# A fused SGU, conformer and SwiGLU block: half 1's group norm centred by rounded parts, first feature tiles in other PSUM banks, row sums by array halves, squares in pairs, and a search over the planner's order

## The chip, the cores and the metric

The kernel runs on one core of a Trainium2 chip. The metric is device time in microseconds of one execution. Four compute engines work side by side, each on an instruction stream of its own: TensorE (PE; its weight loads are listed as PEld), VectorE (DVE), ScalarE (ACT) and GpSimd (POOL). SyncE (SP) issues the transfers. An instruction waits on semaphores for the data or the buffer that it needs, and everything behind it on its engine waits with it.

## The reference

One decoder block for 1024 tokens of width 1024 in float32: two mixers side by side, an output projection, a feed-forward part and a last norm. Cut to what matters here:

```python
cond = silu(c) @ ada_w + ada_b                  # six modulation vectors
h = modulate(rmsnorm(x, norm1_g), shift1, scale1)
u, v, val, gate = split(h @ w_in + b_in)        # 512 columns each
v = layernorm(gelu(v)); w = tril(w_s)           # 8 heads, chunks of 128
y_a = gelu(u) * (einsum('hts,bcshd->bcthd', w, v) + b_s)
y = val * sigmoid(gate)
y = causal_depthwise_conv(y, conv_w, width=31) + conv_b
y_b = silu(layernorm(y in 8 groups of 64 channels))
x = x + gate1 * (concat(rmsnorm(y_a), rmsnorm(y_b)) @ w_out)
h2 = modulate(rmsnorm(x, norm2_g), shift2, scale2)
x = x + gate2 * ((silu(g_ff) * up_ff) @ w_ffn_out)   # g_ff, up_ff = h2 @ w_ffn_in
out = modulate(rmsnorm(x, norm_f_g), shift_f, scale_f)
```

## The kernel before

**Layout.** Activations lie feature-major: eight tiles `x0` to `x7` of 128 features by 1024 tokens, worked on in two halves of 512 tokens, half 0 and half 1. Names carry the half: `pu0_2` is tile 2 of the u projection of half 0.

**Products.** A float32 product is made of three products of rounded operands (fp32r). `weights` and `split` make a rounded copy `hi` on ScalarE (`wh_*`) and the rest, `lo` = raw - hi, on GpSimd or VectorE (`wl_*`). `mm3` (L747 to 749; the same in `product`, L1109) then adds hi x hi, lo x hi and hi x lo in one PSUM bank, each a 512-wide matmul. A few matmuls run on plain float32 operands: the sums of squares, the scale matmuls and the group norm's centring among them.

**Stages.** The first phase multiplies half 0's `h1` with the val and gate weights in eight banks, `p0_0` to `p3_1` (L871 onwards), while weights and modulation rows arrive. `glu` (L819) puts sigmoid on the gate tile (`sg`, L821) and writes into `ypad`. Then come the u projection of half 0 (`pu0_*`), the norm of half 1, half 1's `h1_1` tiles (`modulated`, low parts on GpSimd), `pu1_*`, `spatial_bias` (`rs`), the v projection (`v*`, weights `wl_v_*`), the conv as 31 taps on VectorE (L1047), group norm, the spatial mixing (`pm`, L989), the output projection (`po*`, on `y_a` and `y_b`), val and gate of half 1 (`p10_*`, `p11_*`), and a first part of the feed-forward product (`ah*`). The conv and group norm of half 1 lie beside `ah`. After half 1's output projection and second norm the feed-forward part follows: seven products in place of eight by sums of blocks, in banks `A`, `B` and `C`. The last norm (`ssq_nf`, `rt_nf`, `of`) ends the program.

**What the change touches.**

- `rstd` (L779 on) makes 1/rms. ScalarE squares each tile (L789), groups of them can be added up first (L793), and matmuls of 32 output rows add over the partitions (L797); sqrt, reciprocal (L802, L803), and a matmul that spreads the result to 128 rows (L806). For the norm of half 1, `r1b`, there were eight groups of one tile: 8 x 4 narrow matmuls into `ssq_n1_1`.
- `group_norm` (L1063): for each pair of tiles, a matmul with the centring matrix `gcen` on the copied conv result `s` (L1067; float32, 512 wide), square and copy by ScalarE (L1070, L1071), narrow sums with `gind` (L1074), sqrt and reciprocal `gsd`, a matmul that spreads it (L1082, 64 output rows), product on VectorE (L1085), silu (L1086).
- `spatial_bias` (L848): sums over the rows of the masked weights `wt`. Two float32 matmuls of 512 columns give all eight heads' sums on all 128 rows (L850), and eight VectorE instructions scale and add them (L855), one per head, 64 rows each.
- PSUM: rings of three `mm` banks, two `cv`, two `gn` and one `nrm`. A new tile takes a bank of its ring and waits for that bank's readers; which tile takes which bank follows the planned order. `alloc` gave p0 the `cv` banks, p1 `gn`, p2 and p3_0 `mm`, p3_1 `nrm`; the small `warm` and `ada0` tiles lay in `mm`.

**Order.** Nothing runs in the order in which it is written. `fix_order` (L565) builds a graph of all instructions and lets a list scheduler write an order for each engine and for SP's transfers, forward and backward, for twelve settings of its margins (`MARGINS`). Each result is replayed under eight sets of random delays; the order with the lowest mean is pinned. Its costs are numbers in the file.

Of the kernel before, what the change touches and what calls it, by code (L numbers as in the profile page):

```python
# [7 lines left out]
F32 = mybir.dt.float32  # L8
F32R = mybir.dt.float32r
# [4 lines left out]
P = 128  # L14
S = 1024
D = 1024
# [17 lines left out]
N_FILL = 8  # L34
WARM = (5, 4, 3, 4)
N_POOL_TAPS = (6, 6)

# [16 lines left out]
def tile_order():  # L54
# [20 lines left out]
           (0.02, 0.1, 0.0), (0.015, 0.05, 0.5))  # L75
N_REPLAYS = 8


# [53 lines left out]
def duration(s):  # L132
# [3 lines left out]
    if s.engine == "PE":  # L136
        n, m = s.writes[0].width, s.reads[1].width
        if not s.reads[0].f32:
            t = (n + 32) / 2400 * (0.5 if m == 64 else 1)
        else:  # L140
            k = s.reads[0].box[1] - s.reads[0].box[0]
            t = max({128: 0.219, 32: 0.068}.get(m, 0.109 if k > 64 else 0.055) * n / 128, 0.2 if n < 32 else 0.0)
        return t, t + 0.176, 0
# [35 lines left out]
class Graph:  # L179


    def __init__(self, instructions, edges, stacked, reusing):
        self.steps = []
        uses, live, tiles, order, bank = {}, {}, {}, {}, {}
        for ins in instructions:
# [3 lines left out]
            for operands, written in ((s.reads, False), (s.writes, True)):  # L189
                for o in operands:  # L190
# [7 lines left out]
                    for other, wrote, box in live[o.name]:  # L198
                        if other is not s and meet(box, o.box):
                            if written or wrote or (o.space == "PSUM" and other.engine != s.engine):  # L200
# [24 lines left out]
        self.uses = uses  # L225
        self.tag_of = {name: tag for tag, names in order.items() for name in names}
# [101 lines left out]
class Clock:  # L328
# [164 lines left out]

def replay(g, order, follows, late):

    before = [set(s.before) for s in g.steps]
    for old, new in follows:
        for n in g.first[new]:
            before[n].update(m for m in g.final[old] if m != n)
    done, free, at, begun = [None] * len(g.steps), [0.0] * len(g.steps), {}, [0.0] * len(g.steps)  # L500
    clock, table, place = Clock(True), None, dict.fromkeys(order, 0)

    def arrival(s):
        t = 0.0
        for n in before[s.n]:
            if done[n] is None:
                return None
            p = g.steps[n]
            if (n, s.n) in g.issued:
                t = max(t, begun[n])  # L510
            elif p.engine == s.engine and not p.dma:
                t = max(t, free[n] if p.engine == "PE" else done[n])
            else:
                t = max(t, done[n] + SIGNAL[p.engine])
        return t

    while True:
        best = None
        for e, steps in order.items():
            if place[e] == len(steps):  # L520
                continue
            s = steps[place[e]]
            if s.n not in at:
                t = arrival(s)
                if t is None:
                    continue
                at[s.n] = t
            t = max(clock.free[e], at[s.n])
            if best is None or t < best[0]:
                best = t, e, s  # L530
        if best is None:
            return max(done)
        t, e, s = best
        if s.table not in (None, table):
            table, t = s.table, t + TABLE_LOAD
        begun[s.n] = t
        done[s.n] = clock.run(s, t)[1] + late[s.n]
        if not s.dma:
            clock.free[e] += late[s.n]
        free[s.n] = clock.free[e]  # L540
        place[e] += 1

# [20 lines left out]


def fix_order(tc, edges, stacked, reusing, rounds=5):  # L565

# [3 lines left out]
    for engines, pool, wait in MARGINS:  # L570
        stretch(g, engines, pool)
        order, done, follows = forward(g, list(range(len(g.steps))), wait)
        for _ in range(rounds):
# [8 lines left out]
            if best is None or mean < best[0]:  # L582
                best = mean, order
    for steps in best[1].values():
        for earlier, later in zip(steps, steps[1:]):
# [6 lines left out]
def block_kernel(ctx: ExitStack, tc: tile.TileContext, xT, c, ada0, ada, cols, vbias, bs, wsp,  # L592
# [79 lines left out]
    for h in range(2):  # L672
# [4 lines left out]
        with issue_after(sqrt_table):  # L677
            A.activation(cact[:, hs(h)], cb, AF.Copy)
    warm_bank = mm_bank("warm")

# [145 lines left out]

    wt = front.tile([P, NH, P], F32, name="wt")
# [3 lines left out]
    cstt = front.tile([P, P + 64], F32, name="cstt")  # L831
    gcen, gind = cstt[:, 0:P], cstt[:, P:]

    def load_mixer_operands():
# [9 lines left out]
        A.activation(vsel, col("sel_hl"), AF.Copy)  # L844
        nc.sync.dma_start(cstt, cst)

    def spatial_bias():
        for q in range(2):  # L848
            rs = mm_bank(f"rs{q}")
            PE.matmul(rs, ones.broadcast_to([P, P]), wt[:, 4 * q:4 * q + 4, :], start=True, stop=True)  # L850
# [10 lines left out]
    ada0_bank = mm_bank("ada0")  # L861
    h1 = [[None] * KD, [None] * KD]
# [163 lines left out]
    def conv_pair(half, jp, n_pool, s):  # L1026
# [27 lines left out]
        for j in js:  # L1054
            if n_pool:
                V.tensor_tensor(s[j], s[j], accs[j], op=ALU.add)
            else:
                A.activation(s[j], accs[j], AF.Copy)
        with tc.high_priority():
            group_norm(half, jp, js, s)  # L1060

    def group_norm(half, jp, js, s):
        sqs = {}  # L1063
        bank = {j: gn_bank(f"gn{half}_{j}") for j in js}
        b0, b1 = (bank[j] for j in js)
        for j in js:
            PE.matmul(bank[j], gcen, s[j], start=True, stop=True)  # L1067
        for j in js:
# [68 lines left out]
    with tc.high_priority():  # L1137
        r1b = rstd(x_half(1), D, "n1_1", (1,) * 8, G)
    for k in range(KD):
# [468 lines left out]
```

## Time and profile before

| | |
|---|---|
| median of three runs | 977.72 us (976.61 to 978.66) |
| the profiled execution | 976.81 us |
| its span | 975.1 us |
| mean granted TensorE clock | 0.996 |
| TensorE busy | 959.4 us, 98% |
| VectorE busy | 867.0 us, 89% |
| ScalarE busy | 472.4 us, 48% |
| GpSimd busy | 397.9 us, 41% |
| HBM over the span | 188 GB/s |

The profile is of one execution: 1.71 us of its time lie outside the span. A line of the trace gives start and duration in microseconds, engine, line of the kernel, the tile written and the tiles read, and a count where rows are merged; behind a row may stand, in brackets, how long the engine was idle before it and what released it. Matmuls overlap, so a matmul's cost is read from one start to the next. A float32 matmul is recorded as two.

### The profile page before, as it was taken

To read this page: it belongs to the slowest core of one execution; us is meant where nothing else is said; L and a number is where in the kernel's file an instruction comes from. 1 tells how busy PE (TensorE), PEld (TensorE's weight loads), DVE (VectorE), ACT (ScalarE), POOL (GpSimd) and SP (SyncE) were. 2 spreads that over 40 slices of the span, in tenths; PEclk is the share of its full clock that TensorE was granted. 3 is DMA by queue.
4 is the path that set the end of the run, shared out by engine and by line. 5 is a ranking of instruction groups with operands and counts; after the bars stand their busy time and mean duration, and the time that the engine had idled before them with its cause. 6 is when DMAs were issued, how large, how long until landed. Compare 5 with 4: busy or idle time off the path is not lost.

```text
span 975.1 us, 13473 instructions
## 1 busy us (share of the span) xinstructions
PE 959.4 (98%) x4766; PEld 782.4 (80%) x4766; DVE 867.0 (89%) x1206; ACT 472.4 (48%) x752; POOL 397.9 (41%) x240
## 2 busy tenths in 40 slices
PE   8999999999999999999999999999999999999996
PEld 6877777778878778888888888888888888888875
DVE  5999999899999553799999999999989989969956
ACT  5788466643564653465233333333336437227426
POOL 0069888556453312574454535545443100000113
PEclk9999999999999999999999999999999999999998
DMA  8983451434465424864666667777658937415104
GB/s 324 338 304 101 157 168 65 152 130 140 156 215 185 146 84 166 264 233 140 207 222 239 236 239 248 251 238 233 228 196 284 301 121 266 149 33 168 50 1 173
DMA packets 73682, 184.10 MB, mean 189 GB/s; under 512 B 8208, under 2 KB 10512, under 8 KB 73616
## 3 DMA queue, kind: packets, MB, share of 16 engines
q1 hardware_dynamic: 73616, 183.25, 55.5%
q8 instruction: 37, 0.61, 0.3%
q14 instruction: 29, 0.24, 0.1%
HBM read 142.06 MB, written 41.16 MB: 188 GB/s over the span
## 4 chain that ended last, share of the span: by engine, by line
PE 92%; DVE 4%; DMA 2%; ACT 1%; issue 1%; SPq 0%; DVEq 0%; ACTq 0%
PE B L1109 31%; PE C L1109 19%; PE ah L1109 11%; PE A L1109 4%; PE po L747 3%; PE po L748 3%; PE po L749 3%; PE v L747 2%; PE pu L747 2%; PE v L749 2%; PE pu L748 2%; PE v L748 1%; PE pu L749 1%; PE p L747 1%; PE p L748 1%; PE p L749 1%
## 5 line engine op out<-in xcount | busy, mean ns | idle before, releaser
L1109 PE MATMUL B<-h,w_f 128*128 128x512 f32 x816 | 189.8, 389 | 0.0
L1109 PEld LDWEIGHTS B<-h,w_f 128*128 128x128 f32 x816 | 153.2, 188 | 31.8
L1047 DVE SCALAR_TENSOR_TENSOR cv<-ypad,colt,cv 128x512 f32<-128x512 f32 x216 | 146.7, 744 | 0.2
L1109 PE MATMUL B<-fa,w_d 128*128 128x512 f32 x528 | 124.9, 389 | 0.5 <-DVE x L1465 0.5
L1109 PE MATMUL C<-h,w_f 128*128 128x512 f32 x528 | 123.7, 389 | 0.0
L1109 PEld LDWEIGHTS B<-fa,w_d 128*128 128x128 f32 x528 | 98.9, 188 | 21.5 <-DVE x L1465 0.8
L1109 PEld LDWEIGHTS C<-h,w_f 128*128 128x128 f32 x528 | 99.1, 188 | 20.6
L1109 PE MATMUL ah<-h,wh_a 128*128 128x512 f32 x320 | 101.2, 394 | 0.4 <-ACT sg L821 0.4
L1101 ACT ACTIVATE w_f<-raw_f 128x512 fp32r<-128x512 f32 x68 | 42.5, 630 | 96.9 <-PE B L1109 37.5
L1101 ACT ACTIVATE w_d<-raw_d 128x512 fp32r<-128x512 f32 (+1 forms) x72 | 41.8, 593 | 82.3 <-PE B L1109 33.2
L731 POOL TENSOR_TENSOR wl_a<-raw_a,wh_a 128x1024 fp32r<-128x1024 f32 x20 | 49.1, 2454 | 78.1 <-ACT wh_a L730 78.1
L1404 POOL TENSOR_TENSOR sq_nf<-sq_nf,sq_nf 128x512 f32<-128x512 f32 (+1 forms) x7 | 8.5, 1228 | 166.9 <-ACT sq_nf L1383 162.6
L1102 DVE TENSOR_TENSOR w_f<-raw_f,w_f 128x512 fp32r<-128x512 f32 x68 | 73.0, 1084 | 0.5 <-ACT w_f L1101 0.4
L1109 PEld LDWEIGHTS ah<-h,wh_a 128*128 128x128 f32 x320 | 59.8, 188 | 15.2 <-issue 1.9
L1355 POOL TENSOR_TENSOR x<-x,u 128x512 f32<-128x512 f32 x22 | 37.1, 1688 | 70.3 <-DVE u L1354 42.3
L1109 PE MATMUL C<-fa,w_d 128*128 128x512 f32 (+1 forms) x318 | 64.4, 354 | 0.0
L1109 PE MATMUL ah<-h,wl_a 128*128 128x512 f32 x160 | 62.5, 393 | 0.0
L1109 PEld LDWEIGHTS C<-fa,w_d 128*128 128x128 f32 x318 | 52.6, 189 | 8.8 <-issue 0.4
L1465 DVE SCALAR_TENSOR_TENSOR x<-B,cond,x 128x512 f32<-128x512 f32 x48 | 35.8, 747 | 20.4 <-PE B L1109 20.1
L1102 DVE TENSOR_TENSOR fa<-a,fa 128x512 fp32r<-128x512 f32 x77 | 52.8, 730 | 0.0
L1352 POOL TENSOR_TENSOR x<-x,up 128x512 f32<-128x512 f32 x20 | 32.7, 1633 | 42.2 <-ACT x L1351 42.2
L1101 ACT ACTIVATE fa<-a 128x512 fp32r<-128x512 f32 x77 | 46.1, 626 | 7.2 <-DMA a<-acts 4.0
(258 smaller groups left out, 2130.8 us busy)
## 6 DMA issues: line engine op xcount, KB each, us to landing
acts<-x SPq DMA_DIRECT2D x77, 256.0 KB, 3.0
a<-acts SPq DMA_DIRECT2D x77, 256.0 KB, 4.0
raw_f<-wf SPq DMA_DIRECT2D x32, 512.0 KB, 4.1
ada<-ada SPq DMA_DIRECT2D x24, 512.0 KB, 4.2
x<-ada SPq DMA_DIRECT2D x24, 512.0 KB, 4.1
raw_a<-wf SPq DMA_DIRECT2D x20, 512.0 KB, 3.8
ahead<-ahead SPq DMA_DIRECT2D x40, 256.0 KB, 2.6
raw_o<-wo SPq DMA_DIRECT2D x16, 512.0 KB, 3.5
```

The lines of the kernel that those rows point to most:

```text
L731: lo_eng.tensor_tensor(lo, raw, hi.bitcast(F32), op=ALU.subtract)
L747: PE.matmul(acc, shi, mhi, start=start, stop=False)
L748: PE.matmul(acc, slo, mhi, start=False, stop=False)
L749: PE.matmul(acc, shi, mlo, start=False, stop=stop)
L1047: V.scalar_tensor_tensor(accs[j], src, wc, accs[j], op0=ALU.mult, op1=ALU.add)
L1101: A.activation(dst[:, 0, :], src, AF.Copy)
L1102: lo_eng.tensor_tensor(dst[:, 1, :], src, dst[:, 0, :].bitcast(F32), op=ALU.subtract)
L1109: last_mm = PE.matmul(bank[:, cols], s, m[:, cols], start=first and p == 0 and i == 0, stop=p == n - 1 and i == 2, skip_group_check=True)
L1352: G.tensor_tensor(g0, g0, up0, op=ALU.mult)
L1355: G.tensor_tensor(g1, g1, u2, op=ALU.mult)
L1404: G.tensor_tensor(run, run, t, op=ALU.add)
L1465: V.scalar_tensor_tensor(xs[k][:, part], bank[:, cols], ccol(GATE2, k), xs[k][:, part], op0=ALU.mult, op1=ALU.add)
```

## The change

1. Half 1's centring (`ROUNDED`): ScalarE's copy of the conv result becomes a rounded copy `gh`, VectorE makes the rest `gl`, and two rounded matmuls per tile with a rounded copy of the matrix (`gcr`) take the place of one in float32. `gl` lies in the buffer of `wt`.
2. The first phase's tiles take the `mm` ring first: p0 and p1_0 lie in `mm`, p1_1 and p2_0 in `cv`, p2_1 and p3_0 in `gn`; `warm` and `ada0` lie in `gn`.
3. The row sums are made head by head, each for only the 64 rows that use it, side by side in one bank: eight matmuls of 128 columns, and four VectorE instructions of 128 rows.
4. The squares of half 1's first norm are added in pairs on GpSimd (four additions), so that 16 narrow matmuls remain of 32.
5. The planner: other costs for narrow matmuls and for going in and out of them; readings of PSUM on the same engine count as dependences; the replay is rewritten; and after the choice of margins `climb` makes up to 300 changes of the ranks along the chains that TensorE waits for in the replay, keeping each that lowers the mean.

```diff
+ROUNDED = (False, True)
...
+N_CHANGES = 300
...
-            t += 0.09 if s.partial else 0.12
+            t += 0.18 if s.partial else 0.23
...
+    order = climb(g, lates, *best)
...
-    alloc = [cv_bank] * 2 + [gn_bank] * 2 + [mm_bank] * 3 + [nrm_bank]
+    alloc = [mm_bank] * 3 + [cv_bank] * 2 + [gn_bank] * 2 + [nrm_bank]
...
     def spatial_bias():
-        for q in range(2):
-            rs = mm_bank(f"rs{q}")
-            PE.matmul(rs, ones.broadcast_to([P, P]), wt[:, 4 * q:4 * q + 4, :], start=True, stop=True)
-            for hh in range(4):
-                hd = 4 * q + hh
-                e, hp = hd % 2, hd // 2
-                rows = slice(e * 64, (e + 1) * 64)
-                V.scalar_tensor_tensor(bst[rows, hp, :], rs[rows, hh * P:(hh + 1) * P],
-                                       col("a_ln_b", hp)[rows], bst[rows, hp, :],
-                                       op0=ALU.mult, op1=ALU.add)
+        rs = mm_bank("rs")
+        for hp in range(4):
+            for e in range(2):
+                PE.matmul(rs[e * 64:(e + 1) * 64, hp * P:(hp + 1) * P], ones.broadcast_to([P, 64]),
+                          wt[:, 2 * hp + e, :], start=True, stop=True)
+        for hp in range(4):
+            V.scalar_tensor_tensor(bst[:, hp, :], rs[:, hp * P:(hp + 1) * P], col("a_ln_b", hp), bst[:, hp, :],
+                                   op0=ALU.mult, op1=ALU.add)
...
         for j in js:
-            PE.matmul(bank[j], gcen, s[j], start=True, stop=True)
+            if not ROUNDED[half]:
+                PE.matmul(bank[j], gcen, s[j], start=True, stop=True)
+                continue
+            hi = front.tile([P, H], F32R, tag="ctmp", name=f"gh{half}_{j}", bufs=2)
+            lo = los[:, j - js[0], :]
+            A.activation(hi, src[j], AF.Copy)
+            (V if half else G).tensor_tensor(lo, src[j], hi.bitcast(F32), op=ALU.subtract)
+            PE.matmul(bank[j], gcr, hi, start=True, stop=False)
+            PE.matmul(bank[j], gcr, lo, start=False, stop=True)
...
-        r1b = rstd(x_half(1), D, "n1_1", (1,) * 8, G)
+        r1b = rstd(x_half(1), D, "n1_1", (2,) * 4, G)
```

What the planner and the search make of it is shown at three places. The first is TensorE in the u projection of half 0, where the sums of squares of half 1 are put in (`sq_n1_1_*` the squares, `pu0_2` the products around). Before:

```order
L749 MATMUL pu0_2_694<-h1_0_2_313,wh_u_2_687 128x512
L797 MATMUL ssq_n1_1_765<-sq_n1_1_0_766,ones_92 32x128 x4
L797 MATMUL ssq_n1_1_765<-sq_n1_1_1_772,ones_92 32x128 x4
L747 MATMUL pu0_2_694<-h1_0_3_355,wh_u_2_687 128x512
L797 MATMUL ssq_n1_1_765<-sq_n1_1_2_778,ones_92 32x128 x4
L797 MATMUL ssq_n1_1_765<-sq_n1_1_3_784,ones_92 32x128 x4
L797 MATMUL ssq_n1_1_765<-sq_n1_1_4_790,ones_92 32x128 x4
L797 MATMUL ssq_n1_1_765<-sq_n1_1_5_796,ones_92 32x128 x4
L797 MATMUL ssq_n1_1_765<-sq_n1_1_6_802,ones_92 32x128 x4
L797 MATMUL ssq_n1_1_765<-sq_n1_1_7_808,ones_92 32x128 x4
L748 MATMUL pu0_2_694<-h1_0_3_355,wl_u_2_688 128x512
```

After, on TensorE at the same place:

```order
L858 MATMUL pu0_2_695<-h1_0_3_356,wh_u_2_688 128x512
L859 MATMUL pu0_2_695<-h1_0_3_356,wl_u_2_689 128x512
L908 MATMUL ssq_n1_1_767<-sq_n1_1_0_768,ones_92 32x128 x4
L908 MATMUL ssq_n1_1_767<-sq_n1_1_2_777,ones_92 32x128 x4
L908 MATMUL ssq_n1_1_767<-sq_n1_1_4_786,ones_92 32x128 x4
L908 MATMUL ssq_n1_1_767<-sq_n1_1_6_795,ones_92 32x128 x4
L860 MATMUL pu0_2_695<-h1_0_3_356,wh_u_2_688 128x512
```

The sums stood in two pieces with one product between them, and now stand in one piece, one product later.

The second is ScalarE at the end of the first phase (`sg*_0` are the sigmoids that read the gate tiles p0_1 to p3_1; `wh_u_2` is the rounding of a weight for `pu0_2`; `sq_n1_1_*` are squares of half 1). Before:

```order
L789 ACTIVATE sq_n1_1_0_766<-x0_75 128x512
L789 ACTIVATE sq_n1_1_1_772<-x1_76 128x512
L730 ACTIVATE wh_u_2_687<-raw_u_2_685 128x1024
L821 ACT_TABLE_LOAD
L821 ACTIVATE sg0_0_555<-p0_1_198,colt_74 128x512
L821 ACTIVATE sg1_0_558<-p1_1_200,colt_74 128x512
L821 ACTIVATE sg2_0_561<-p2_1_202,colt_74 128x512
L821 ACTIVATE sg3_0_564<-p3_1_204,colt_74 128x512
```

After, on ScalarE:

```order
L954 ACTIVATE vb_132<-vb_raw_760 128x512
L900 ACTIVATE sq_n1_1_1_770<-x1_76 128x512
L900 ACTIVATE sq_n1_1_2_777<-x2_77 128x512
L932 ACT_TABLE_LOAD
L932 ACTIVATE sg0_0_556<-p0_1_199,colt_74 128x512
L932 ACTIVATE sg1_0_559<-p1_1_201,colt_74 128x512
L932 ACTIVATE sg2_0_562<-p2_1_203,colt_74 128x512
L932 ACTIVATE sg3_0_565<-p3_1_205,colt_74 128x512
```

The rounding of `wh_u_2` stood ahead of the table load and the sigmoids, and now stands behind them.

The third is TensorE in half 1's output projection, around the scale matmuls of its conv branch (`rt_b1`) and the first products with `y_b1`. Before:

```order
L747 MATMUL po1_2_3187<-y_a1_3_2591,wh_o1_2_3181 128x512
L806 MATMUL ssq_b1_3116<-rt_b1_3132,colt_74 128x128 x4
L748 MATMUL po1_2_3187<-y_a1_3_2591,wl_o1_2_3182 128x512
L749 MATMUL po1_2_3187<-y_a1_3_2591,wh_o1_2_3181 128x512
L747 MATMUL po1_0_3185<-y_b1_0_3141,wh_o1_0_3169 128x512
```

After, on TensorE:

```order
L860 MATMUL po1_2_3192<-y_a1_0_2567,wh_o1_2_3186 128x512
L917 MATMUL ssq_b1_3121<-rt_b1_3137,colt_74 128x128 x4
L858 MATMUL po1_2_3192<-y_a1_1_2572,wh_o1_2_3186 128x512
L859 MATMUL po1_2_3192<-y_a1_1_2572,wl_o1_2_3187 128x512
L860 MATMUL po1_2_3192<-y_a1_1_2572,wh_o1_2_3186 128x512
L858 MATMUL po1_2_3192<-y_a1_2_2577,wh_o1_2_3186 128x512
L859 MATMUL po1_2_3192<-y_a1_2_2577,wl_o1_2_3187 128x512
L860 MATMUL po1_2_3192<-y_a1_2_2577,wh_o1_2_3186 128x512
L858 MATMUL po1_2_3192<-y_a1_3_2582,wh_o1_2_3186 128x512
L859 MATMUL po1_2_3192<-y_a1_3_2582,wl_o1_2_3187 128x512
L860 MATMUL po1_2_3192<-y_a1_3_2582,wh_o1_2_3186 128x512
L858 MATMUL po1_0_3190<-y_b1_0_3146,wh_o1_0_3174 128x512
```

Two products with `y_a1` stood between the scale matmuls and the first product with `y_b1`; now nine do.

More of the change, by code (lines that the diff above doesn't have):

```diff
@@ L491, in backward, with replay @@
     return tail
-def replay(g, order, follows, late):
-    before = [set(s.before) for s in g.steps]
+def replay(g, order, follows, late, times=None):
+    if g.waits is None:
+        g.waits = []
+        for s in g.steps:
+            links = []
+            for n in s.before:
+                p = g.steps[n]
+                if (n, s.n) in g.issued:
+                    links.append((n, 0, 0.0))
+                elif p.engine == s.engine and not p.dma:
+                    links.append((n, 1 if p.engine == "PE" else 2, 0.0))
+                else:
+                    links.append((n, 2, SIGNAL[p.engine]))
+            g.waits.append(links)
+    more = {}
@@ L497, in replay @@
     for old, new in follows:
         for n in g.first[new]:
[L499 to L503, printed above, removed]
+            links = more.setdefault(n, [])
+            for m in g.final[old]:
+                if m != n:
+                    p = g.steps[m]
+                    if p.engine == g.steps[n].engine and not p.dma:
+                        links.append((m, 1 if p.engine == "PE" else 2, 0.0))
+                    else:
+                        links.append((m, 2, SIGNAL[p.engine]))
@@ L504, in arrival @@
+    count = len(g.steps)
+    begun, free, done = [None] * count, [None] * count, [None] * count
+    values = begun, free, done
+    waits, run, steps = g.waits, None, g.steps
+    clock, table = Clock(True), None
+    run, engine_free = clock.run, clock.free
+    queues = [(e, iter(ss)) for e, ss in order.items()]
+    heads = [[e, it, next(it, None), None] for e, it in queues]
+    heads = [h for h in heads if h[2] is not None]
+    def arrival(n):
         t = 0.0
-        for n in before[s.n]:
-            if done[n] is None:
-                return None
[L508 to L514, printed above, removed]
@@ L515, in arrival @@
-        return t
[L517 to L524, printed above, removed]
+        for m, kind, signal in waits[n]:
+            v = values[kind][m]
+            if v is None:
+                return None
+            v += signal
+            if v > t:
+                t = v
+        if n in more:
+            for m, kind, signal in more[n]:
+                v = values[kind][m]
+                if v is None:
+                    return None
+                v += signal
+                if v > t:
+                    t = v
@@ L534, in replay @@
         if s.table not in (None, table):
             table, t = s.table, t + TABLE_LOAD
-        begun[s.n] = t
-        done[s.n] = clock.run(s, t)[1] + late[s.n]
+        n = s.n
+        begun[n] = t
+        done[n] = run(s, t)[1] + late[n]
         if not s.dma:
-            clock.free[e] += late[s.n]
-        free[s.n] = clock.free[e]
-        place[e] += 1
+            engine_free[e] += late[n]
+        free[n] = engine_free[e]
+        best[2], best[3] = next(it, None), None
+        if best[2] is None:
+            heads.remove(best)
@@ L544, in lateness @@
+    if times is not None:
+        times[:] = begun, done
+    return max(done)
 def lateness(g, seed):
@@ L562, in stretch, with climb, waiting, links @@
         s.issue, s.finish, s.port = issue * (1 + k), finish + issue * k, port * (1 + k)
+def climb(g, lates, mean, order, follows, rank, margins):
+    import random
+    r = random.Random(1)
+    engines, pool, wait = margins
+    def waiting(late):
+        times, stalls, end = [], [], 0.0
+        replay(g, order, follows, late, times)
+        begun, done = times
+        for s in order["PE"]:
+            if begun[s.n] > max(end + 0.05, 5.0):
+                stalls.append((begun[s.n] - end, s.n))
+            end = begun[s.n] + s.issue
+        return begun, done, stalls
+    def links():
+        previous, waits = {}, {}
+        for steps in order.values():
+            previous.update((b.n, a.n) for a, b in zip(steps, steps[1:]))
+        for old, new in follows:
+            for m in g.first[new]:
+                waits.setdefault(m, []).extend(g.final[old])
+        return previous, waits
+    def chain(n, depth):
+        found = []
+        for _ in range(depth):
+            ends = [(done[m], m, True) for m in sorted(g.steps[n].before) + waits.get(n, []) if m != n]
+            if n in previous:
+                p = g.steps[previous[n]]
+                ends.append((begun[p.n] + p.issue, p.n, False))
+            if not ends:
+                break
+            _, n, data = max(ends)
+            found.append((n, data))
+        return found
+    best = [replay(g, order, follows, late) for late in lates]
+    seen, joined = {}, None
+    for _ in range(N_CHANGES):
+        i = r.randrange(len(lates))
+        if i not in seen:
+            seen[i] = waiting(lates[i])
+        begun, done, stalls = seen[i]
+        previous, waits = joined = joined or links()
+        n = r.choices([n for _, n in stalls], [t for t, _ in stalls])[0]
+        found = chain(n, r.choice((1, 2, 3, 5, 8, 12, 20)))
+        by, changed = r.choice((0.5, 1.0, 2.0, 4.0, 8.0)), list(rank)
+        if r.random() < 0.5:
+            for m, _ in [(n, True)] + found:
+                changed[m] -= by
+        else:
+            for m, data in found:
+                if not data:
+                    changed[m] += by
+        stretch(g, engines, pool)
+        trial = forward(g, changed, wait)
+        stretch(g, 0.0, 0.0)
+        ends = []
+        for i, late in enumerate(lates):
+            ends.append(replay(g, trial[0], trial[2], late))
+            if sum(ends) > sum(best[:i + 1]) + (1.0 if i < 2 else 2.0):
+                break
+        else:
+            if sum(ends) < sum(best) - 1e-6:
+                best, order, follows, rank, seen, joined = ends, trial[0], trial[2], changed, {}, None
+    return order
@@ L678, in block_kernel @@
             A.activation(cact[:, hs(h)], cb, AF.Copy)
[L679 removed]
+    warm_bank = gn_bank("warm")
     def keep_warm(count, ins):
```

44 lines of the change are left out of this document (27 added, 17 removed).

## The prediction

> **What bounds the kernel now.** I read the page first (busy shares and the chain that ended last), then the waits of TensorE, then busy time by windows, and last the chain and the timeline for the price of each kind of matmul.
>
> ```profile
> PE 959.4 (98%) x4766; PEld 782.4 (80%) x4766; DVE 867.0 (89%) x1206; ACT 472.4 (48%) x752; POOL 397.9 (41%) x240
> PE   8999999999999999999999999999999999999996
> PE 92%; DVE 4%; DMA 2%; ACT 1%; issue 1%; SPq 0%; DVEq 0%; ACTq 0%
> ```
>
> TensorE is busy for 959.4 of the span's 975.1 us and makes 92% of the chain. Only the first and the last slice are not full, so nearly every microsecond must come out of TensorE's own work, or out of the few waits inside:
>
> ```profile
> PE c L675 <- ACT cvec L667: 2.8, 1, 2.8
> PE ssq_nf L1413 <- DVE rt_nf L1411: 1.9, 1, 1.9
> PE po L747 <- ACT y_b L1005: 1.1, 1, 1.1
> PE pu L747 <- ACT sg L821: 0.8, 1, 0.8
> PE ah L1109 <- ACT sg L821: 0.4, 1, 0.4
> ```
>
> The first belongs to the head and the second to the tail. The three that a new order in the front could remove are `po` 1.1, `pu` 0.8 and `ah` 0.4, 2.3 us together. The windows show where they lie (columns: PE, PEld, DVE, ACT, POOL busy):
>
> ```profile
> 50.00:75.00 25.00, 24.18 (x107) 19.66 (x106) 24.67 (x24) 20.63 (x29) 17.40 (x9) 1.00 0.87 304
> 75.00:100.00 25.00, 25.00 (x168) 20.00 (x167) 24.67 (x38) 20.68 (x32) 21.34 (x16) 1.00 0.23 73
> 100.00:125.00 25.00, 25.00 (x106) 19.54 (x105) 24.75 (x43) 11.91 (x19) 22.89 (x10) 1.00 0.55 186
> 250.00:275.00 25.00, 24.63 (x127) 18.61 (x126) 24.39 (x37) 18.16 (x28) 8.93 (x5) 1.00 0.52 179
> 350.00:375.00 25.00, 23.90 (x115) 19.17 (x115) 13.34 (x18) 9.29 (x13) 0.47 (x1) 1.00 0.35 116
> ```
>
> The clock stands at 1.00 in all of them. VectorE is as full as TensorE up to 125 us, and GpSimd is 21 to 23 of 25 us busy there; both matter below. Later, in the feed-forward part, TensorE runs without a gap, so what it gains in the front should arrive at the end whole.
>
> **The change part by part.** Prices from the chain. The trace records a float32 matmul as two, so x48 below is 24 matmuls, x32 is 16 and x4 is 2:
>
> ```profile
> 76.37 1.57 PE ssq_n L797 x48
> 109.62 1.72 PE rs L850 x4
> 148.80 1.90 PE gn L1082 x32
> 333.74 1.72 PE gn L1067 x4
> 463.33 8.16 PE B L1109 x36
> ```
>
> So a 512-wide matmul costs 8.16/36 = 0.227 us on rounded operands and 1.72/2 = 0.86 in float32; a 128-column one costs 1.57/24 = 0.065 with 32 output rows and 1.90/16 = 0.119 with 64. Going over to such shapes and back has a price too (timeline of TensorE; first number start, second duration):
>
> ```profile
> 74.98 0.39 PE L749 MATMUL pu<-h,wh_u 128*128 128x512 f32 x1
> 75.30 0.64 PE L797 MATMUL ssq_n<-sq_n,ones 128*32 128x128 f32 x16
> 75.87 0.50 PE L747 MATMUL pu<-h,wh_u 128*128 128x512 f32 x1
> 76.30 1.64 PE L797 MATMUL ssq_n<-sq_n,ones 128*32 128x128 f32 x48
> 77.87 0.50 PE L748 MATMUL pu<-h,wl_u 128*128 128x512 f32 x1
> 78.20 0.40 PE L749 MATMUL pu<-h,wh_u 128*128 128x512 f32 x1
> ...
> 111.12 0.49 PE L747 MATMUL v<-wh_v,h 128*128 128x512 f32 x1
> 111.46 0.39 PE L748 MATMUL v<-wh_v,h 128*128 128x512 f32 x1
> ```
>
> From one start to the next, `pu` at 74.98 takes 0.32 instead of 0.227: 0.09 to go in. The one at 77.87 takes 0.33: about 0.11 to come out. A visit to narrow shapes thus costs 0.2 beside its matmuls. Coming out of float32 (111.12 to 111.46) costs 0.11 as well.
>
> (a) Centring of half 1. Four float32 matmuls (0.86 each) become eight rounded ones: 4 x (0.86 - 0.453) = 1.63 saved, and two exits from float32, 0.22. ScalarE exchanges a copy for another, and makes one rounded copy of the centring matrix early, which nothing waits for; VectorE gets four subtractions, priced below.
>
> (b) Squares in pairs. Before, 32 narrow matmuls in two visits: 0.57 + 1.57 and twice 0.2 = 2.54. After, 16 in one visit: 16 x 0.065 + 0.2 = 1.25. Saved 1.28.
>
> (c) Row sums by halves. Before 1.72 + 0.11 = 1.83; after, eight 64-row matmuls, 8 x 0.119 = 0.95, in two visits as the order has it, 0.4. Saved 0.48. The Trainium skill (TensorEngine Tiling (Array Packing), Tiling Modes, Key Properties) says that changing the tiling mode drains the array, which speaks against cutting a wide matmul into narrow ones in two visits. The trace agrees that there is a price, 0.09 in and 0.11 out; the rows above bound a whole drain by 0.39 - 0.227 = 0.16 each way, with which this item would still save about 0.24.
>
> (d) The search merges visits. Counting in the order from the first `pu` to the feed-forward part, narrow visits go from 28 to 26 and wide float32 ones from 14 to 10. Edits (a) to (c) explain three float32 visits and one narrow one more; the remaining three narrow and one float32 visit less are the search's: 3 x 0.2 + 0.11 = 0.7.
>
> TensorE's own work in the front thus falls by 1.85 + 1.28 + 0.48 + 0.7 = 4.3.
>
> (e) Waits. `pu`:
>
> ```profile
> 57.88 1.06 ACT L730 ACTIVATE wh_u<-raw_u 128x1024 fp32r<-128x1024 f32 x1 [2.35 <-DMA raw_u<-wu]
> 58.96 1.28 ACT L821 ACT_TABLE_LOAD   x1
> 60.26 2.42 ACT L821 ACTIVATE sg<-p,colt 128x512 f32<-128x512 f32 x4
> ```
>
> Before, the first `pu` takes its bank from tile p2_1, whose reader is the third `sg`, and ScalarE reaches the `sg`s late: it waited 2.35 us for a weight, rounded it, loaded its table, and the third of four `sg`s ended at about 62.1. After, that rounding is behind the `sg`s and the bank comes from p0_1, read by the first one. The banks of p0 are complete before the last two tiles' matmuls, so ScalarE can start about 1 us earlier and needs one `sg` and not three. The 0.8 goes. On SP's queue the loads of half 1's tiles x2 to x5 move ahead of that weight's load, which waits for a raw buffer anyway, and x6 and x7 behind the next weight and two conditioning loads; the sums that read their squares start at 75.30, so I count this as nothing.
>
> `po`, at the first product with `y_b`:
>
> ```profile
> 354.50 1.05 PE L806 MATMUL ssq_b<-rt_b,colt 128*128 128x128 f32 x8
> 355.31 0.48 PE L748 MATMUL po<-y_a,wl_o 128*128 128x512 f32 x1
> 355.62 0.40 PE L749 MATMUL po<-y_a,wh_o 128*128 128x512 f32 x1
> 357.12 0.50 PE L747 MATMUL po<-y_b,wh_o 128*128 128x512 f32 x1 [1.10 <-ACT y_b L1005]
> ```
>
> From the start of the scale matmuls, `y_b` takes 357.12 - 354.50 = 2.62 us by way of VectorE and ScalarE, and two products cover 1.5 of them. After, nine products stand there: 0.81 + 0.11 + 9 x 0.227 = 2.96 us, more than 2.62. The 1.1 goes, if the scale itself is in time: between the sum `ssq_b1` and the scale matmuls stand 12 instead of 13 products, so some 0.2 of slack is lost.
>
> `ah`: a bank freed by the last `sg`. After, p11_3 is completed before the rest of p10_3, so its `sg` runs sooner; but the chain from the scale of half 0's second norm to the first `ah` loads the sigmoid table on ScalarE in its midst, and I see little slack. I take the 0.4 as gone and allow 0.4 for such new waits over the whole program.
>
> (f) Tail. Two more visits (+0.4), but the last scale sits earlier among the last products, with three and not five output scalings ahead of its reciprocal on VectorE, which shortens the wait of 1.9 by some part. Taken as nothing, -1 to +1 for the range.
>
> (g) What is added on other engines. Rows for the four subtractions and the four additions (minimum/median/maximum ns), and the last tap of half 1's conv with the centring of its second pair:
>
> ```profile
> L1102 DVE TENSOR_TENSOR fa<-a,fa 128x512 fp32r<-128x512 f32 x77 | 52.8, 730 | 0.0
> L793 POOL TENSOR_TENSOR sq_b<-sq_b,sq_b x5: 1277/1801/2285, 193.9 to 348.7; 128x512 f32<-128x512 f32 x5
> 317.96 0.75 DVE L1047 SCALAR_TENSOR_TENSOR cv<-ypad,colt,cv 128x512 f32<-128x512 f32 x1
> 333.57 1.88 PE L1067 MATMUL gn<-s,cstt 128*128 128x512 f32 x4
> ```
>
> VectorE: +4 x 0.73 = 2.9, between 260 and 335 us. Up to 275 it has half a microsecond free, but the last tap ends at 318.7 and the second pair is centred from 333.57, since both centring banks still hold the first pair. These 15 us hide the subtractions; without them they would cost up to 2.9. The scalings of the row sums become four instead of eight, which I count as nothing. GpSimd: +4 x 1.28 = 5.1 (up to 4 x 2.29 = 9.1), three of them ahead of the low parts of `wu`'s third and fourth weight; its idle time from 75 to 125 is 3.66 + 2.11 = 5.8 us. Following GpSimd's new queue with such durations, `wu`'s low parts are done 3 to 5 us before their products and the last of `wv` about 2 us before. So I cost the additions at nothing; it is the least certain cover of this sum, and rival 4 is what it costs when gone.
>
> Sum: -4.3 (work) - 2.3 (waits) + 0.4 (new waits) + 0 (tail) = -6.2, rounded to -6. Against the profiled execution's 976.81 that is 970.8; the median of the runs shown, 977.72, is 0.9 above that execution and would give 971.7. I forecast 971.2, the case's own range 969 to 973.2.
>
> **Rivals.**
>
> 1. New waits in place of the old. `y_b`, the first `ah` and the first `pu` are each close to their data; if they wait as before, 2.3 + 0.4 of the sum stay and the time is 976.8 - 4.3 + 0.4 = 972.9. With 1.4 more lost in the tail and the merged visits, 974.3. For it: the margin at `y_b` is 0.3 us. Against: for `pu` it is over 1 us. Chance 0.18.
>
> 2. The change doesn't do what it says: the search's order wins nothing on the chip, neither merged visits nor waits, and only edits (a) to (c) count: 976.8 - 3.6 = 973.2, with small losses up to 975. Chance 0.05.
>
> 3. VectorE's chain is the true limit of the front: conv, group norm and `y_b` finish when they did, with 2.9 us more on them, and all that TensorE saves before 350 us becomes wait at `y_b`. Only what lies behind remains: about 976 to 978. For it: VectorE is full to 125 us and the wait at `y_b` is the largest inside. Against: the 15 us between the last tap and the centring. Chance 0.06.
>
> 4. Slower: GpSimd becomes the bound from 55 to 115 us. Its queue is served in order; three of the new additions stand ahead of the weights' low parts and the half's low parts of `h`. The idle 5.8 takes up four additions of 1.28, but beside VectorE the two slow each other:
>
> ```profile
> 50.53 5.98 POOL L731 TENSOR_TENSOR wl_u<-raw_u,wh_u 128x1024 fp32r<-128x1024 f32 x2 [48.96 <-PE p L749]
> 50.82 3.43 DVE L703 SCALAR_TENSOR_TENSOR ada<-ada,cact 128x1024 f32<-128x1024 f32 x1
> ```
>
> Two weights took 5.98/2 = 2.99 each here, and the scaling beside them 3.43. If each addition takes 2.29 and no idle time is left for any of it, 9.1 us arrive at TensorE: 970.8 + 9.1 = 979.9. It decides from about 9 us of wait at `pu` or `v`. The Trainium skill (GPSIMD Engine Reference, Specifications) says that GpSimd's access to SBUF is shared with VectorE, contending with its instructions that have two SBUF inputs; the rows agree, and it speaks against more sums on GpSimd just here. Against: all 5.8 us of idle time would have to be lost as well. Chance 0.03.
>
> **How the numbers follow.** Forecast 0.68, rivals 0.18, 0.05, 0.06 and 0.03. About 0.2%, 2 us, is what a measurement of this kernel can tell from no change, so faster is below 975.8 and slower above 979.7. The forecast, rival 1 and rival 2 are faster: 0.68 + 0.18 + 0.05, less 0.01 for what of them lies above, 0.90. Same: rival 3 and that 0.01, 0.07. Slower: rival 4, 0.03. The range leaves out 0.07 below (more waits gone than counted) and about 0.1 above (rivals 3 and 4): 968.7 to 975.2.
>
> **What would show it.** In the profile of the changed kernel TensorE's busy time should be about 4 us lower; the chain should show the narrow `ssq_n` matmuls of half 1 at about 1.05 us in one piece, `rs` at 0.95 in two, and each pair's centring at 0.91. The wait list should have lost `pu` 0.8 and `po` 1.1; what stands there instead with more than 0.5 us, above all `po` behind `y_b`, `pu` behind a weight, or `v` behind `wl_v`, is rival 1, 3 or 4. Windows from 75 to 125 with TensorE under 24.5 would be rival 4. The span is 1.71 below the execution's time, so the forecast is wrong if the span is above 971.5 or below 967.3.

## The result and the profile after

The changed kernel takes 971.37 us (median of 4 runs, 971.11 to 972.04), the kernel before 977.37 beside it (4 runs, 976.61 to 978.66): 0.9938 of the time, 95% interval 0.9921 to 0.9956, or 6.0 us less. The prediction said 971.2. The profiled execution of the changed kernel took 971.62 us, its span 969.9.

The page after, the same rows as before (busy time by engine, busy tenths of TensorE, the chain that ended last):

```profile
PE 955.8 (99%) x4746; PEld 783.1 (81%) x4746; DVE 864.2 (89%) x1206; ACT 471.2 (49%) x753; POOL 408.2 (42%) x244
PE   8999999999999999999999999999999999999996
PE 89%; DVE 1%; ACT 1%; POOL 0%; issue 0%; DVEq 0%; ACTq 0%; POOLq 0%
```

TensorE lost 3.6 us of busy time and is still the bound; GpSimd gained 10.3. The waits of TensorE after:

```profile
PE c L786 <- ACT cvec L778: 2.9, 1, 2.9
PE ssq_nf L1534 <- DVE rt_nf L1532: 1.0, 1, 1.0
PE ssq_n L917 <- DVE rt_n L914: 0.7, 1, 0.7
PE ssq_b L908 <- POOL sq_b L904: 0.5, 1, 0.5
PE ssq_nf L1515 <- POOL sqs_nf L1525: 0.5, 1, 0.5
PE ssq_nf L1515 <- POOL sq_nf L1525: 0.4, 1, 0.4
...
PE p L858 <- ACT sg L932: 0.3, 1, 0.3
```

`po` 1.1, `pu` 0.8, `ah` 0.4 and `B` 0.5 are gone. New are 0.7 at the scale of half 1's first norm, 0.5 for a GpSimd sum of squares in half 1's conv branch, 0.3 for a sigmoid, and two in the tail, at `ssq_nf`. The windows, with the columns of the prediction's, show the first of them at 75 to 100:

```profile
50.00:75.00 25.00, 25.00 (x139) 20.43 (x137) 24.30 (x27) 21.31 (x29) 21.01 (x10) 1.00 0.88 310
75.00:100.00 25.00, 24.31 (x114) 19.94 (x111) 24.94 (x37) 19.98 (x32) 22.91 (x17) 1.00 0.21 65
...
350.00:375.00 25.00, 25.00 (x112) 20.46 (x111) 14.24 (x19) 10.89 (x14) 2.40 (x1) 1.00 0.41 138
```

The starts of the same matmuls in the two timelines tell where the time went. The third column is the changed kernel, profiled once more in the fifth experiment.

| stretch of TensorE | before | after | after, again |
|---|---|---|---|
| start to first `p` | 17.49 | 16.90 | 16.63 |
| first `p` to first `pu` | 44.66 | 43.66 | 43.65 |
| first `pu` to first `v` | 48.97 | 48.13 | 47.17 |
| first `v` to first `ah` | 157.21 | 157.61 | 157.62 |
| first `ah` to first `po` on `y_b1` | 88.79 | 84.94 | 84.97 |
| from there to first `B` | 81.56 | 81.48 | 81.48 |
| first `B` to the last scale matmuls | 528.03 | 528.33 | 528.32 |

The stretches repeat to some hundredths, except two. The head took 16.63 to 17.26 in six profiles with the changed kernel's order of it, and so its 0.6 or 0.9 doesn't count safely for the change. The stretch from `pu` to `v` was 0.96 longer in the first profile than in the second, and the experiments come back to it. The first profile also ends later: its last scale matmuls took 1.87 us and those of the second 1.10, because the granted clock fell to half in their midst (0.79 in the mean from 960 to 962).

### The profile page after: what moved, and what is told of

It reads as the page before. It is cut to its first block, busy times and chain, and to the rows that moved or that the text cites. A ratio compares the mean times of both kernels' runs of the same rounds, so it can differ in the third digit from the quotient of the medians.

```text
span 969.9 us, 13444 instructions
## 1 busy us (share of the span) xinstructions
PE 955.8 (99%) x4746; PEld 783.1 (81%) x4746; DVE 864.2 (89%) x1206; ACT 471.2 (49%) x753; POOL 408.2 (42%) x244
## 4 chain that ended last, share of the span: by engine, by line
PE 89%; DVE 1%; ACT 1%; POOL 0%; issue 0%; DVEq 0%; ACTq 0%; POOLq 0%
PE B L1230 31%; PE C L1230 18%; PE ah L1230 11%; PE A L1230 4%; PE po L858 3%; PE po L859 3%; PE po L860 3%; PE v L858 2%; PE v L860 2%; PE v L859 2%; PE p L858 1%; PE p L860 1%; PE p L859 1%; PE pu L859 1%; PE pu L860 1%; PE pu L858 1%
## 5 line engine op out<-in xcount | busy, mean ns | idle before, releaser
L1223 DVE TENSOR_TENSOR w_f<-raw_f,w_f 128x512 fp32r<-128x512 f32 x68 | 65.4, 969 | 0.1
L1223 DVE TENSOR_TENSOR w_d<-raw_d,w_d 128x512 fp32r<-128x512 f32 (+1 forms) x72 | 47.8, 676 | 1.8 <-ACT w_d L1222 1.8
```

The source lines that it names most:

```text
L1223: lo_eng.tensor_tensor(dst[:, 1, :], src, dst[:, 0, :].bitcast(F32), op=ALU.subtract)
```

## The experiments

Where an order was kept, the steps of every engine were written out as the changed kernel has them (or the kernel before, in the seventh), new steps stand at the places of those that they replace, and no planner ran. Where another search or a new plan is measured, its order was made beforehand with the setting that the diff shows, and written out in the same way. The experiments come in three sets; each set was measured on one chip, with the kernel before beside it.

**First set: undo one part, order kept** (the kernel before: 977.08).

Half 1's centring in float32:

```diff
-ROUNDED = (False, True)
+ROUNDED = (False, False)
```

> The changed kernel with its order of every engine written out and kept; only half 1's centring is undone (a ScalarE copy, one float32 matmul per tile at the place of the two rounded ones; the four VectorE subtractions and the rounded centring matrix are gone). Theory, TensorE is the bound and the saved matmul time arrives at the end: 4 x (0.86 - 0.453) + 2 x 0.11 = 1.85 us slower than the changed kernel, 973.2. Rival, VectorE's chain of conv, group norm and y_b sets the end of the front: taking four subtractions of 0.73 off it pays for the longer matmuls, within 0.5 us of the changed kernel, 971.4 to 971.9, or faster.

Measured: 971.71 us, against 970.39 and 970.15 for the third and fourth experiments, whose edits change nothing that shows. The stretch from `ah` to `po` is 86.48, 1.51 longer than in the changed kernel's second profile. The timelines of TensorE, first with float32, then the changed kernel:

```profile
267.65 1.88 PE L1181 MATMUL gn<-s,cstt 128*128 128x512 f32 x4
268.96 0.79 PE L1230 MATMUL ah<-h,wh_a 128*128 128x512 f32 x1
269.60 0.40 PE L1230 MATMUL ah<-h,wl_a 128*128 128x512 f32 x1
```

```profile
268.35 0.39 PE L1187 MATMUL gn<-gh,gcr 128*128 128x512 f32 x1
...
269.27 0.39 PE L1230 MATMUL ah<-h,wh_a 128*128 128x512 f32 x1
269.50 0.39 PE L1230 MATMUL ah<-h,wl_a 128*128 128x512 f32 x1
```

From the first centring to the second product behind it: 1.95 in float32, 1.15 with parts, 0.80 for each pair. The saving is real and arrives, so VectorE's chain isn't the limit. It is 1.5 to 1.6 and not 1.85: the 0.11 of coming out of float32 lies inside the 1.72 of the two matmuls (1.95 - 0.227), and I had counted it twice.

Row sums over the whole array:

```diff
-                PE.matmul(rs[e * 64:(e + 1) * 64, hp * P:(hp + 1) * P], ones.broadcast_to([P, 64]),
-                          wt[:, 2 * hp + e, :], start=True, stop=True)
+            PE.matmul(rs, ones.broadcast_to([P, P]), wt[:, 4 * q:4 * q + 4, :], start=True, stop=True)
```

> The changed kernel with its order kept; only the row sums are undone (two float32 matmuls of 512 columns at the place of the second visit, eight VectorE scalings of 64 rows at the place of four). Theory, two visits to narrow shapes cost 0.2 each: 1.83 - 1.35 = 0.48 us slower, 971.9. Rival, a change of shape drains the array in full, 0.16 each way: 0.24 slower, 971.6. Rival, the scalings on VectorE count, not the matmuls: 1.4 us slower.

Measured: 970.53 us, and `pu` to `v` is 47.34, 0.17 longer than in the changed kernel's second profile. The two visits by halves, in the changed kernel, and then the whole one:

```profile
102.07 0.44 PE L964 MATMUL rs<-wt,ones 128*64 128x128 f32 x4
102.44 0.50 PE L859 MATMUL pu<-h,wl_u 128*128 128x512 f32 x1
...
107.88 0.88 PE L964 MATMUL rs<-wt,ones 128*64 128x128 f32 x12
108.69 0.50 PE L858 MATMUL v<-wh_v,h 128*128 128x512 f32 x1
```

```profile
106.56 1.88 PE L963 MATMUL rs<-wt,ones 128*128 128x512 f32 x4
108.22 0.49 PE L858 MATMUL v<-wh_v,h 128*128 128x512 f32 x1
108.55 0.39 PE L859 MATMUL v<-wh_v,h 128*128 128x512 f32 x1
```

By halves, 0.37 for two matmuls and 0.81 for six, where 0.119 each would make 0.24 and 0.71: a visit costs 0.1 more than its matmuls and its way in and out. With 0.2 for each way in and out that is 1.58, against 1.76 whole (1.99 for the visit and the product behind it, less 0.227). The part brings 0.17, not 0.48. The rival with a whole drain was nearer with 0.24, but its reason isn't shown: the extra 0.1 lies between the first and the last start of the visit. VectorE's scalings don't count.

The old banks for the first phase (`warm` and `ada0` go back to `mm` with them):

```diff
-    alloc = [mm_bank] * 3 + [cv_bank] * 2 + [gn_bank] * 2 + [nrm_bank]
+    alloc = [cv_bank] * 2 + [gn_bank] * 2 + [mm_bank] * 3 + [nrm_bank]
```

> The changed kernel with its order kept; only the banks of the first phase's tiles are as before (p0 in the conv banks, p1 in the group-norm banks, p2 and p3_0 in the product banks). As the prediction has it, the first u product waits for the third sigmoid again: up to 0.8 us slower, 972.2. Second theory, after reading the changed kernel's trace: the sigmoids run from 58.43 to 61.0 there, the third ends at 60.3, and the u product starts at 60.56; then moving the weight's rounding behind the sigmoids took the wait away by itself and the banks give nothing: within 0.2, 971.4.

Measured: 970.39 us, no slower. Its timeline of ScalarE, and then of TensorE:

```profile
57.12 1.28 ACT L932 ACT_TABLE_LOAD   x1
58.41 1.85 ACT L932 ACTIVATE sg<-p,colt 128x512 f32<-128x512 f32 x3
```

```profile
60.83 0.39 PE L858 MATMUL pu<-h,wh_u 128*128 128x512 f32 x1
```

The third sigmoid ends at 60.26 and the first `pu` starts at 60.83 without a wait. Behind an order that puts the weight's rounding after the sigmoids, the banks give nothing. Whether the planner would find that order with the old banks wasn't tried.

The reciprocal ahead of its neighbour in VectorE's order (the two exchanged, nothing else):

> The changed kernel with one exchange of neighbours in VectorE's order: the reciprocal of half 1's first norm ahead of the conditioning scaling that stands before it and takes 2.15 us beside GpSimd. Theory, the new wait of 0.69 us at the scale matmuls is in full on the chain, as TensorE has no spare time: 0.7 faster, 970.7. Rival, TensorE would wait as long a little later, for half 1's h tiles or a weight's low part: no change, 971.4.

Measured: 970.15 us, and `pu` to `v` 47.17, exactly as in the first and third experiments, which kept the old place. There was nothing to gain: neither of those two has the wait of 0.69. So this run doesn't tell whether such a wait would reach the end in full.

**Second set: the order, and one part alone** (the kernel before: 976.95).

The changed kernel again:

> The changed kernel again, every engine in the order that it had, on the chip of the three that follow, as their measure. Both theories: 6 us faster than the kernel before, 0.994 of it. In its trace the wait of 0.69 at the scale matmuls of half 1's first norm (79.87) is there again if it belongs to the order; it is gone, and the stretch from the first u product to the first v product takes 47.2 instead of 48.1, if it came from a conditioning load that arrived late in one execution.

Measured: 969.70 us (969.66 to 971.2), 0.9930 of the kernel before, interval 0.9918 to 0.9943. The wait isn't there. VectorE around the reciprocal, first in the changed kernel's first profile, then here:

```profile
72.52 1.70 DVE L814 SCALAR_TENSOR_TENSOR ada<-ada,cact 128x1024 f32<-128x1024 f32 x1 [0.63 <-DMA ada<-ada]
...
76.79 2.15 DVE L814 SCALAR_TENSOR_TENSOR ada<-ada,cact 128x1024 f32<-128x1024 f32 x1
...
78.87 0.94 DVE L914 RECIPROCAL rt_n<-rt_n 128x128 f32<-128x128 f32 x1
```

```profile
71.64 1.30 DVE L814 SCALAR_TENSOR_TENSOR ada<-ada,cact 128x1024 f32<-128x1024 f32 x1
...
75.50 1.97 DVE L814 SCALAR_TENSOR_TENSOR ada<-ada,cact 128x1024 f32<-128x1024 f32 x1
...
77.40 0.94 DVE L914 RECIPROCAL rt_n<-rt_n 128x128 f32<-128x128 f32 x1
```

In the first profile a conditioning load (`ada`) came 0.63 late and the two scalings took 0.58 longer, and VectorE's queue handed both on to the reciprocal. The order doesn't bring it: every engine has the same order here. Whether the three unprofiled executions of the first result had it too isn't known; at 971.1 to 972.0 they were as long as the profiled one, and four of the five here were 970.5 or less.

The search switched off:

```diff
-N_CHANGES = 300
+N_CHANGES = 0
```

> The changed kernel with the search switched off; the planner's new costs and all hand edits stay. Theory of the prediction, the search merges visits and takes the waits away: 0.7 + 2.3 us slower than the changed kernel, 974. Rival, from the order without the search: the weight's rounding stands behind the sigmoids and nine products stand ahead of y_b there too, with one narrow visit more, so that the planner's new costs and the banks did it: at most 0.6 slower, 971.

Measured: 971.75 us, 2.05 slower than the changed kernel beside it, between the two. Its waits of TensorE:

```profile
PE ssq_nf L1534 <- DVE rt_nf L1532: 1.0, 1, 1.0
PE ssq_nf L1515 <- POOL sqs_nf L1525: 0.6, 1, 0.6
PE ssq_b L908 <- POOL sq_b L904: 0.5, 1, 0.5
PE B L1230 <- DVE x L1586: 0.5, 1, 0.5
```

The three waits of the front that the first theory gave to the search are gone without it. Its worth is elsewhere: half lies in the tail (529.38 from the first `B` to the last scale matmuls, against 528.32), where the planner alone does worse than the planner before (528.03), the rest in small waits and a visit.

Pairs alone, in the kernel before, its order kept:

```diff
-        r1b = rstd(x_half(1), D, "n1_1", (1,) * 8, G)
+        r1b = rstd(x_half(1), D, "n1_1", (2,) * 4, G)
```

> The kernel before with one part of the change: squares of half 1's first norm in pairs on GpSimd, 16 narrow matmuls in two visits of 4 and 12, everything else in the order of before; the last two additions stand behind two sums of the conv on GpSimd. Theory, only TensorE's time counts: 16 matmuls of 0.065 fewer, 1.05 us faster than the kernel before, 976.0. Rival, GpSimd is the bound there and the additions (1.3 to 2.3 each) delay wu's low parts or the scale: no gain or slower, 977 to 979.

Measured: 982.99 us, 6.0 slower than the kernel before (ratio 1.006, interval 1.0047 to 1.0072). GpSimd's timeline, TensorE's, and three windows (the granted clock stands before the last two columns):

```profile
73.24 3.51 POOL L1042 TENSOR_TENSOR s<-s,cp 128x512 f32<-128x512 f32 x2
76.70 3.47 POOL L793 TENSOR_TENSOR sq_n<-sq_n,sq_n 128x512 f32<-128x512 f32 x2
```

```profile
78.03 0.65 PE L797 MATMUL ssq_n<-sq_n,ones 128*32 128x128 f32 x8 [1.63 <-POOL sq_n L793]
80.23 0.66 PE L797 MATMUL ssq_n<-sq_n,ones 128*32 128x128 f32 x8 [1.55 <-POOL sq_n L793]
...
81.40 0.63 PE L749 MATMUL pu<-h,wh_u 128*128 128x512 f32 x1
81.83 0.63 PE L747 MATMUL pu<-h,wh_u 128*128 128x512 f32 x1
```

```profile
77.00:78.00 1.00, 0.00 (x0) 0.00 (x0) 1.00 (x1) 0.98 (x2) 1.00 (x2) 1.00 0.87 328
78.00:79.00 1.00, 0.65 (x8) 0.20 (x8) 1.00 (x3) 0.81 (x1) 1.00 (x1) 0.53 0.22 86
...
84.00:85.00 1.00, 1.00 (x4) 0.80 (x3) 0.86 (x2) 0.69 (x1) 1.00 (x1) 0.56 0.00 0
```

The last two additions queue behind two sums of the conv on GpSimd, and the sums of squares wait 1.63 and 1.55 for them. That is 3.2 us, and the stretch from `pu` to `v` grew by 5.0 although 1.05 of matmul time had gone: the granted clock fell from 1.00 to 0.50 as the first wait ended, at about 78.05, stayed there until about 84.9 (0.53 and 0.56 are the means of the windows in which it changed), and `pu`'s products went at 0.43 instead of 0.227 each. So the rival in which GpSimd decides is a true one, and the time lies 4 us above even its 977 to 979, which hold no price for the clock. In the changed kernel's order three additions stand ahead of the third and fourth weight's low parts and none behind the conv's sums, and its lists have no wait for them.

A search of 1500 steps:

```diff
-N_CHANGES = 300
+N_CHANGES = 1500
```

> The changed kernel with a search of 1500 steps in place of 300, its order written out. Theory: it has one narrow visit fewer in the front and one narrow and one wide float32 visit fewer in the tail, 0.4 to 0.6 us, and the waits that are left (0.26, 0.55, 0.39, 0.52, 1.02) are the most that it could take: 969 to 970. Rival, orders that are better in the replay are not better on the chip: 970.4 to 971.4.

Measured: 967.83 us (4 runs), 1.87 less than the changed kernel beside it and more than either theory gave. The gain is more than visits: the waits for a sigmoid (0.26), for `sq_b` (0.55) and for `sq_nf` (0.39) went as well.

**Third set: edits without their order, another order, and further** (the kernel before: 977.66).

The three hand edits of the front undone, banks and planner and search as changed, the order planned anew:

> The changed kernel with its planner, its search and its banks, but with half 1's centring, the row sums and the squares as before; the order is planned anew. Theory, the hand edits' matmul time is saved in full: 1.6 (centring, from the trace of the experiment that undid it) + 1.33 (squares, 2.54 before and 1.21 after) + 0.17 (row sums) = 3.1 us slower than the changed kernel, 972.8 to 973.5. Rival, the order is all: at most 1 us slower, under 971.

Measured: 979.66 us (12 runs), slower than the kernel before (1.002, interval 1.0011 to 1.0028). This run can't say what the edits are worth, since its new order differs everywhere. From `pu` to `v` and from `ah` to `po` it is 2.44 and 1.16 longer than the changed kernel, 3.6 together and near the 3.1 expected. The other 6 us of the 10 lie where none of the three edits does, and so with the new order: 3.6 up to the first `pu`, with a wait of 1.28 at the first `p` and a granted clock of 0.84 from 15 to 20 and 0.82 from 20 to 25; 1.2 from the first `v` to the first `ah`; and 1.3 behind the first `po` on `y_b1`.

Another seed for the search:

```diff
-    r = random.Random(1)
+    r = random.Random(2)
```

> The changed kernel, its search of 300 steps begun with another random seed. Theory, the order is good to a few tenths and the result of the change doesn't hang on one lucky search: within 1 us of the changed kernel, 969 to 971. Rival, the first seed was lucky: like the kernel without a search, 971.7 or slower.

Measured: 970.10 us, 0.9923 of the kernel before (interval 0.9911 to 0.9935): a second seed gives the same, so the change doesn't hang on the first.

Both halves centred by parts:

```diff
-ROUNDED = (False, True)
+ROUNDED = (True, True)
...
-            lo = los[:, j - js[0], :]
+            lo = los[:, j - js[0], :] if half else tmp(f"gl{half}_{j}", F32R)
```

> The changed kernel with both halves centred by rounded parts (half 0's rest in the ring of temporaries, made by GpSimd; four more ScalarE copies), searched for 800 steps. Theory, TensorE is the bound: another 1.6 us of matmul time, 1 to 2 faster than the search of 1500 steps alone, 966 to 967. Rival, GpSimd and ScalarE are full where half 0 is centred (GpSimd 21 of 25 us), and four subtractions of 1.3 to 2.3 turn into waits: 968 or slower.

Measured: 969.72 us, the rival's time. TensorE's timeline shows why it isn't 967:

```profile
189.93 0.51 PE L861 MATMUL p<-h,wh_vg 128*128 128x512 f32 x1 [1.49 <-ACT sg L935]
```

The matmul time is saved, but a wait of 1.49 for a sigmoid, for which ScalarE is late among its other work, takes most of it back. A longer search might remove that wait; it wasn't tried.

A search of 4000 steps:

> The changed kernel with a search of 4000 steps. Theory, what a search can still take are the waits of the tail and a visit or two: 0.2 to 1 us faster than 1500 steps, 967 to 967.7. Rival, better only in the replay: 967.8 or slower.

Measured: 967.73 us (4 runs), 0.9897 of the kernel before, interval 0.9885 to 0.9910. This order and the one of 1500 steps beat both kernels, by about 2 us of the changed one; between the two there is nothing to tell.

## Why the prediction was right, point by point

The frame held: TensorE is the bound, and what the front saved arrived at the feed-forward part. Up to the first `B` the second profile is 7.16 us earlier than before, 0.86 of it in the head, so 6.3 against the 6.2 summed. The tail, taken as nothing, cost 0.3.

That the first median came within 0.2 us of the forecast is luck: the same kernel gave 6.0 us less at first and 7.25 less in the fifth experiment. Some terms were mis-sized too, and they balanced.

- (a) Centring: 1.5 to 1.6, not 1.85. The step that failed is the exit from float32, added to a price that already held it.
- (b) Squares: 1.28 forecast. One visit of 1.01 with its 0.2 stands in the profile, 1.21 against 2.54: 1.33. Right. Its condition, that GpSimd keeps up, was the least certain cover, and the seventh experiment shows what it costs when gone. Rival 4 had the engine and its queue right; what TensorE waited for there was the additions themselves, not the weights' low parts. Whether it strikes depends on the order.
- (c) Row sums: 0.17, not 0.48, for the same double exit and for 0.1 more in each narrow visit.
- (d) Merged visits: there, three narrow ones fewer between `ah` and `po`, but not the search's, as they are there without it too. Whether the planner's new costs, its other changes or the banks merge them wasn't separated. They are worth more than the 0.6 forecast. One of the merged pairs, before and then in the second profile:

```profile
330.76 1.09 PE L1082 MATMUL gn<-gsd,colt 128*64 128x128 f32 x16
331.78 0.50 PE L1109 MATMUL ah<-h,wh_a 128*128 128x512 f32 x1
```

```profile
325.44 1.97 PE L1203 MATMUL gn<-gsd,colt 128*64 128x128 f32 x32
327.33 0.73 PE L1230 MATMUL ah<-h,wh_a 128*128 128x512 f32 x2
```

Eight matmuls took 1.02 from start to start, and sixteen in one visit 1.89, 0.15 less than twice 1.02. With 0.2 for the way in and out that is 0.35 for each visit, 1.0 for the three. The float32 visit merged away, 0.11 in the sum, brought nothing: its price was that same exit.
- (e) Waits: `pu`, `po` and `ah` went as forecast, but their size was read from the idle time that the profile gives, and from one start to the next a wait costs more. `pu` and `ah` before:

```profile
60.94 0.39 PE L749 MATMUL p<-h,wh_k 128*128 128x512 f32 x1
62.15 0.50 PE L747 MATMUL pu<-h,wh_u 128*128 128x512 f32 x1 [0.82 <-ACT sg L821]
62.49 0.40 PE L748 MATMUL pu<-h,wl_u 128*128 128x512 f32 x1
```

```profile
271.06 1.88 PE L1067 MATMUL gn<-s,cstt 128*128 128x512 f32 x4
273.31 0.50 PE L1109 MATMUL ah<-h,wh_a 128*128 128x512 f32 x1 [0.37 <-ACT sg L821]
273.65 0.40 PE L1109 MATMUL ah<-h,wl_a 128*128 128x512 f32 x1
```

Two products at `pu` took 1.55 where 0.45 is normal, so that wait was worth 1.1. The rows at `ah` took 2.59, where the first experiment has 1.95 for the same work: 0.6. `po`, in the prediction's rows, was worth 1.4. That is 3.1 and not 2.3. The new waits for a sigmoid and for `sq_b`, read so, cost 0.5 and 0.6, 1.1 and not the 0.4 allowed. Both readings err the same way, so the net is 2.0 against 1.9 forecast. The reason for `pu` was half wrong: the rounding behind the sigmoids does it, not the bank.
- (g) The four subtractions on VectorE cost nothing that shows: undoing them and the centring together made the kernel slower by almost all of the matmul time.
- Rival 1: the wait of 0.7 in the first profile looked like it, and came with a late load, not with the order.
- Rivals 2 and 3: the waits and the visits did go, with the search or without it, and the first experiment speaks against VectorE's chain as the limit.

Added again with these sizes, TensorE's work falls by 1.55 + 1.33 + 0.17 + 1.0 = 4.1 and the waits by 2.0: 6.1, against 6.3 measured up to the first `B`. From `ah` to `po` the terms meet the 3.82 measured: 1.5 for the centring, 1.0 for the visits, 1.9 for the two waits gone and -0.6 for the new one.

Left open is how much of the 6 us each hand edit would bring with an order of its own; in the run for that a worse order hides it. The order kept gives 1.5 and 0.17 for two of them, the trace 1.33 for the third.

## What to carry to other kernels

Where one engine runs without gaps, a change is worth its busy time there plus the waits that go, and both can be summed from start-to-start times to a few tenths; take prices from one start to the next with the same neighbour behind, or an exit is counted twice, and take a wait so too, as the idle time shown was about 0.3 short of it at four of the five waits here. Work moved to an engine beside it is free only if its place in that engine's queue is chosen with it: the same four additions are part of a kernel that is 6 us faster, and alone made the kernel before 6 us slower. To undo one part, keep the order; a planner that plans anew can change more than the part.

## What the hardware showed that was not expected

One wait of 1.63 us was followed by a TensorE clock of one half. In the seventh experiment the granted clock was at 0.50 from about 78.05, when the second wait, of 1.55, had not begun, to about 84.9, 6.8 us in all; products took 0.43 instead of 0.227, and 3.2 us of waiting cost about 6. In the ninth a wait of 1.28 that ended at 18.89 was enough: the clock was at one half from about 18.4 to 21.8, 3.4 us. That the second wait of the seventh doubled the time is likely, but not shown. But in the eleventh the wait of 1.49 left it at 1.00, as the wait of 1.1 at `po` did before. So the length of a wait alone doesn't decide; what does wasn't tested here. The Trainium skill (TensorE: Matmul & The Clock Gate, What's actually happening) has two clock states, the slower after an idle window of about 3.4 us; here waits of less than half of that were enough twice. The Trainium skill (TensorE: Matmul & The Clock Gate, Wait — 56ns, not 53.3ns?) gives 426.7 ns from start to start for 512 columns in the slower state; this trace agrees, with 0.43. A price list of waits should therefore not be linear.
